# The joining of a DMA-turned SwiGLU tile, moved nine weight units on and tied behind a split in ScalarE's order

## The chip, the cores and the metric

The kernel runs on one core of a Trainium2 chip. The metric is the device time of one execution in microseconds (us). A core has five engines, each with its own queue of instructions that runs in the order in which it was built: TensorE (PE, the matmuls), VectorE (DVE), ScalarE (ACT), GpSimd (POOL) and SyncE (SP, which here only issues DMAs). ScalarE and GpSimd issue DMAs too. An instruction that has to wait on its engine holds up all that stand behind it there.

## The reference

Two decoder layers on a sequence of 256 tokens with a width of 2048. Each layer is a mixer (sparse attention and latent attention side by side, one output projection), a layer norm, a SwiGLU and a second layer norm:

```python
def _swiglu(x, w_gate, w_up, w_down):
    h = jax.nn.silu(jnp.einsum('bsd,df->bsf', x, w_gate)) * jnp.einsum('bsd,df->bsf', x, w_up)
    return jnp.einsum('bsf,fd->bsd', h, w_down)

def reference(x, positions, w_in, ...):
    for i in range(DEPTH):
        mix = _hybrid_mixer(x, positions, w_in[i], ...)
        x = _layer_norm(ALPHA * x + mix, ln1_g[i], ln1_b[i])
        ffn = _swiglu(x, w_gate[i], w_up[i], w_down[i])
        x = _layer_norm(ALPHA * x + ffn, ln2_g[i], ln2_b[i])
    return x
```

All is float32. The hidden width is 5632. The change touches only how the hidden tile of the SwiGLU gets from the gate/up products to the down products.

## The kernel before

**Weight units.** Every matmul takes its operands in two parts, a high part `wh` (rounded to the matmul's format by ScalarE, line 428) and a low part `wl` (what is left, by VectorE, line 429). A weight unit is a tile of 128x1024 (512 KB): two slices of 128 rows with 512 columns each. It is loaded into `raw` by SP, split by `split`, and multiplied: `wh` by the high part of the other operand, `wl` by the high part, `wh` by the low part. `raw` has ten buffers in the SwiGLU, `wh` and `wl` have seven each (`UNITS` 5 and `MORE` 2), so a split waits for the buffer that was used seven units back.

**The SwiGLU.** The 5632 hidden columns are taken in 11 blocks of 512. For a block, `gate_up` makes the gate and up products of 256 tokens by quads of units: a quad stands for a 2x2 group of blocks and is done either plainly or by seven products in place of eight (Winograd's form of Strassen's scheme), for which three units are sums that VectorE or an accumulating DMA makes (lines 1145 to 1159). In some quads the sums are read ready-made from a scratch in HBM. A quad is seven products of six matmuls (`p1 p2 p3 p6 p7 p4 p5`), a block four quads. With the last quad, ScalarE copies product p1 out of its bank into tile `e` (line 1136), and VectorE combines the seven products into `g` and `e` (line 1127). Then `hidden` or `hidden_by_dma` makes silu(gate) times up (lines 1021 to 1026) and the transposed hidden tile `hT` in two parts.

**Turning the tile.** Blocks 0, 2, 4, 6 and 8 of each layer are turned by DMA (`hidden_by_dma`), ten in all. Since the DMA transpose takes elements of two bytes, ScalarE first parts the words into half words (line 1050, into `e`), two DMA transposes are issued on ScalarE's queue (line 1055, from `e` into `g` or `silu`), ScalarE joins the half words again (line 1060, two instructions, into `e`), and a split makes `hT`. Tiles `e` and `silu` (the tag of `g` too) have one buffer each. The other blocks are turned by TensorE (`transpose4`).

**Down.** Ahead of the gate/up of block fc from 2 on, `down_half` multiplies two earlier blocks by half of the columns of `w_down`: eight units, 12 matmuls each. Its sums lie in banks 0 to 3, and ScalarE copies them out with `d` (line 1210), two behind the sixth unit and two behind the eighth. The gate/up products use banks 0 to 3 too: p1 bank 0, p5 bank 1, p6 bank 2, p7 bank 3. So the first product of a block waits until the second pair of `d` has been read out.

**The order.** `tick()` is called once per unit or so, and tasks such as `hidden_by_dma` are generators that are advanced by it: `yield n` means that the next piece is written down n ticks later. The text's order is not the engines' order: a scheduler that models times takes, on each engine, what it holds to be ready, by priority. In the order that it makes, the join of line 1060 stood one or two instructions behind the transposes, whatever was yielded in the text.

Of the kernel before, what the change touches and what calls it, by code (L numbers as in the profile page):

```python
# [28 lines left out]
AF = mybir.ActivationFunctionType  # L29
# [34 lines left out]
BYK = 3  # L64
SOON = 200
FIRSTD = 2
LAND = 7
T2, T2MORE = 4, 6
ALLFROM, SETSFROM, EARLY = 3, 4, 0

# [16 lines left out]
def hybrid_trunk(ctx: ExitStack, tc: tile.TileContext, x, xt_in, pos, w_in, g_cq, g_ckv, w_uq,  # L87
                 w_ukv, w_o, ln1_g, ln1_b, ln1_T, w_gu, w_down, ln2_g, ln2_b, ln2_T, out):
    nc = tc.nc
# [7 lines left out]
    def nm(s):  # L97
        uid[0] += 1
        return f"{s}{uid[0]}"
# [55 lines left out]
    def f(ap):  # L155
        return ap.bitcast(F32)
# [15 lines left out]
    def load_xT(u):  # L172

        if u == 3:
            load_pos()
        elif u == 5:
            gbTs.extend(load_gbT(v[0], True) for v in (ln1_T, ln2_T))
        elif u == 7:
            not_until_now(pos_f)
        s = t2([P, NT, KU, P], "xs")  # L180
        nc.sync.dma_start(s, xt_in[u])
        for t in range(NT):
            split(*x_parts(xT[t], KU * u, KU), s[:, t])
# [45 lines left out]
    def rope_tables():  # L229
# [10 lines left out]
        magic = 1.5 * 2.0 ** 23  # L240
        two_pi = 2.0 * math.pi
        parts, rest = [], two_pi
        for bits in (8, 8, 8):
            e = math.floor(math.log2(rest)) + 1 - bits
# [82 lines left out]
    def some(key, have, more):  # L327

        if phase["name"] == "more":
            phase[key] = phase.get(key, 0) + 1  # L330
            if phase[key] * more % (have + more) < more:
                return phase["pool"], more
        return sb, have
# [18 lines left out]
    latest = {}  # L352
# [7 lines left out]
    def parts(raw, n, own=None, pieces=1):  # L360

        if own is not None:
            wh, wl = own[:, 0], own[:, 1]
        else:
            pool, bufs = some("n", UNITS, MORE)
            wh = pool.tile([P, KU * C], F32R, name=nm("wh"), tag="wh", bufs=bufs)
            wl = pool.tile([P, KU * C], F32R, name=nm("wl"), tag="wl", bufs=bufs)
        latest["wh"] = wh
        for i in range(pieces):
            sl = slice(i * n // pieces, (i + 1) * n // pieces)  # L370
            split(wh[:, sl], wl[:, sl], raw[:, sl])
        return wh[:, :n].rearrange("p (k c) -> p k c", k=KU), wl[:, :n].rearrange("p (k c) -> p k c", k=KU)

    def load_unit(src, n, pieces=1):

        return parts(load_raw(src, n), n, None, pieces)
# [48 lines left out]
            nc.tensor.transpose(psum[:, i * P:(i + 1) * P], s, ident)  # L425

    def split(hi, lo, src):
        nc.scalar.activation(hi, src, AF.Copy)  # L428
        nc.vector.tensor_tensor(lo, src, f(hi), op=ALU.subtract)  # L429

    def xlhs(xT):
        return lambda t, k: tuple(m[:, 0, :] for m in x_parts(xT[t], k, 1))
# [130 lines left out]
    def attend(logits_of, scale, bias, v_of, oh, ol, h0, wait=3):  # L563


        lgs = []
        lp = att()
        logits_of(h0, [[lp[:, j, 0:P], lp[:, j, P:3 * P]] for j in range(2)])
        for t in range(NT):
            n = P * (t + 1)  # L570
            lg = t2([P, 2, n], "lg")
            nc.vector.scalar_tensor_tensor(lg, lp[:, :, t * P:t * P + n], scale,
                                           bias[t].unsqueeze(1).to_broadcast([P, 2, n]), op0=ALU.mult, op1=ALU.add)
            for j in range(2):
                softmax_head(lg[:, j, :], t, n)
            lgs.append(lg)
        yield wait
        prs = []
        for j in range(2):
            tp = trp()  # L580
            transpose4([lgs[0][:, j, :], lgs[1][:, j, 0:P], lgs[1][:, j, P:]], tp)
            pr = t2([P, 3 * P], "pr")
            nc.scalar.activation(pr, tp[:, :3 * P], AF.Copy)
            prs.append(pr)
        yield 1
        op = trp()
        for j, pr in enumerate(prs):
            v0, v1 = v_of(h0 + j)
            ov = op[:, j * S:(j + 1) * S]
            mm(ov, v0, pr[:, 0:S], start=True, stop=False)  # L590
            mm(ov[:, P:], v1, pr[:, S:], start=False, stop=True)
        split(oh.rearrange("p j t -> p (j t)"), ol.rearrange("p j t -> p (j t)"), op)


    def layer(l, xT, norms, last):
# [327 lines left out]
        for c in range(D // C):  # L923
            o = proj([(w_o[l, c, k // KU], range(k, k + KU)) for k in first], olhs, C)
            for t in range(NT):
                sl = xt[t][:, c * C:(c + 1) * C]
# [7 lines left out]
        def last_pass(unit, ks, lhs, then, by, halve=False):  # L934


            us = []
            two = many([P, 2, 2, KU * C])
            for c in range(D // C):
                own = two[:, c] if c < 2 else t8([P, 2, KU * C], F32R, "own")  # L940
                us.append([load_unit(unit(c, ks[0]), KU * C), parts(load_raw(unit(c, ks[1]), KU * C), KU * C, own)])
            for t in range(NT):
                for c in range(D // C):
                    n = C // 2 if halve and t and c == D // C - 1 else C
                    for v in range(0, C, n):
                        o = acc()[:, :n]
                        for i, k0 in enumerate(ks):
                            wh, wl = (w[:, :, v:v + n] for w in us[c][i])
                            for j in range(KU):
                                h, lo = lhs(t, k0 + j)  # L950
                                mm(o, h, wh[:, j, :], start=i == 0 and j == 0, stop=False)
                                mm(o, h, wl[:, j, :], start=False, stop=False)
                                mm(o, lo, wh[:, j, :], start=False, stop=i == len(ks) - 1 and j == KU - 1)
                            tick()
                        sl = xt[t][:, c * C + v:c * C + v + n]
                        with tc.high_priority(offset=SOON):
                            nc.vector.scalar_tensor_tensor(sl, o, by, sl, op0=ALU.mult, op1=ALU.add)
                then(t)
# [54 lines left out]
        def own_words(name):  # L1013

            return phase["pool"].tile([P, NT, C], F32, name=nm(name), tag=name, bufs=1)

        def times_silu(gs, us):

            s = own_words("silu") if isinstance(gs, list) else gs
            for t in range(NT):  # L1020
                nc.scalar.activation(s[:, t, :], gs[t] if isinstance(gs, list) else gs[:, t, :], AF.Silu)
            if isinstance(us, list):
                for t in range(NT):
                    nc.vector.tensor_tensor(s[:, t, :], s[:, t, :], us[t], op=ALU.mult)
            else:
                nc.vector.tensor_tensor(s, s, us, op=ALU.mult)
            return s
# [11 lines left out]
        def words(v):  # L1039

            return v.rearrange("p t c -> p (t c)")

        def hidden_by_dma(gs, us, hT):


            s = times_silu(gs, us)
            e = own_words("e") if isinstance(us, list) else us
            yield 1
            for t in range(NT):
                nc.scalar.activation(e[:, t, :].bitcast(U16).rearrange("p (h c) -> p h c", h=2),  # L1050
                                     s[:, t, :].bitcast(U16).rearrange("p (c h) -> p h c", h=2), AF.Copy)
                yield 1
            turned = words(s).bitcast(U16).rearrange("p (k t) -> p k t", t=S)
            for t in range(NT):
                nc.scalar.dma_start_transpose(turned[:, :, t * P:(t + 1) * P], e[:, t, :].bitcast(U16))
                yield 1
            yield LAND
            whole = words(e).bitcast(U16).rearrange("p (w h) -> p h w", h=2)
            for h in range(2):
                nc.scalar.activation(whole[:, h, :], turned[:, 4 * h:4 * h + 4, :].rearrange("p k t -> p (k t)"), AF.Copy)  # L1060
                yield 1
            split(hT[:, 0], hT[:, 1], words(e).rearrange("p (k t) -> p k t", t=S))

# [169 lines left out]
        def spawn_hidden(fc, g, u):  # L1233
            hT = t8([P, 2, 4, S], F32R, "hT")
            held.append((fc, hT, spawn(hidden_by_dma(g, u, hT) if by_dma(fc) else
                                       hidden(g, u, hT, 3, 2 if fc + 1 < FIRSTD else 4))))
# [103 lines left out]
```

## Time and profile before

| what | us |
|---|---|
| median of 3 runs | 2234.0 (2231.7 to 2241.35) |
| the profiled execution | 2222.58 |
| its span, first to last instruction | 2220.8 |
| TensorE busy in it | 2135.7 |
| VectorE busy | 1862.9 |
| ScalarE busy | 1351.8 |
| mean granted TensorE clock | 0.984 |

Waits are listed as "who waited <- what released it: us in total, times, longest". In a timeline a row is start, duration, engine, line, operation, out <- in; behind it in brackets the idle time of the engine just ahead and what ended it. ACTq is a DMA issue on ScalarE's queue, PEld a weight load of TensorE. In a window row the columns are the stretch, its length, then for PE, PEld, DVE, ACT and POOL the busy time and number of instructions, the granted TensorE clock, the DMA engines' busy share and GB/s.

### The profile page before, as it was taken

How to read it: one execution, taken by the hardware profiler on the slowest of the kernel's cores; microseconds unless marked ns; L12 is line 12 of the kernel's file. 1: busy time of each engine (PE TensorE's matmuls, PEld its weight loads, DVE VectorE, ACT ScalarE, POOL GpSimd, SP SyncE). 2: the span in 40 equal slices, each digit the busy share in tenths (PEclk: the TensorE clock that was granted, in tenths of full speed). 3: DMA queues.
4: the chain of work that ended last, by engine and by line, in shares of the span. 5: the costliest groups of instructions: out<-in, count | busy, mean ns of one | idle time of the engine just before them, and what ended most of it. 6: DMA issues, size and time to landing. Idle time of an engine off the chain costs nothing.

```text
span 2220.8 us, 28336 instructions
## 1 busy us (share of the span) xinstructions
PE 2135.7 (96%) x9862; PEld 1766.8 (80%) x9862; DVE 1862.9 (84%) x2349; ACT 1351.8 (61%) x1732; POOL 334.5 (15%) x527
## 2 busy tenths in 40 slices
PE   9999999999998989989999999999999989899898
PEld 7888888878786868878888888888778868688686
DVE  7697767899897979989867967679989979799897
ACT  6555545666775656666655554466666756566763
POOL 1223220110111100110013122101111111110111
PEclk9999999999999999999999999999999999999999
DMA  8688787689889888988667887867889998989894
GB/s 306 217 294 285 278 309 264 180 240 272 242 278 222 276 235 282 289 240 248 208 180 259 293 302 270 313 213 221 241 245 277 285 217 264 231 278 277 240 308 127
DMA packets 183888, 566.59 MB, mean 255 GB/s; under 512 B 39377, under 2 KB 39681, under 8 KB 183105
## 3 DMA queue, kind: packets, MB, share of 16 engines
q1 hardware_dynamic: 110736, 398.38, 51.2%
q0 software_dynamic: 51600, 160.77, 28.4%
q10 hardware_dynamic: 21408, 5.64, 2.7%
q8 instruction: 77, 1.26, 0.2%
q14 instruction: 67, 0.54, 0.1%
HBM read 506.51 MB, written 31.46 MB: 242 GB/s over the span
## 4 chain that ended last, share of the span: by engine, by line
PE 74%; DVE 9%; DMA 7%; ACT 5%; issue 5%; ACTq 0%; POOL 0%; SPq 0%; DVEq 0%; POOLq 0%
PE acc L392 8%; PE acc L393 8%; PE acc L394 8%; PE gu_p L1085 5%; PE gu_p L1087 5%; PE gu_p L1088 5%; PE acc L1203 4%; PE acc L1204 4%; DMA g<-e 4%; PE acc L1202 4%; DVE wl L429 4%; PE gu_c L1085 3%; PE gu_c L1087 3%; PE gu_c L1088 3%; ACT wh L428 2%
## 5 line engine op out<-in xcount | busy, mean ns | idle before, releaser
L429 DVE TENSOR_TENSOR wl<-raw,wh 128x1024 fp32r<-128x1024 f32 (+2 forms) x925 | 1091.5, 1213 | 269.6 <-ACT wh L428 267.3
L428 ACT ACTIVATE wh<-raw 128x1024 fp32r<-128x1024 f32 (+2 forms) x925 | 948.4, 1050 | 575.3 <-PE acc L394 145.5
L392 PE MATMUL acc<-wh,xhl 128*128 128x512 f32 (+1 forms) x756 | 297.8, 395 | 0.0
L394 PE MATMUL acc<-wh,xhl 128*128 128x512 f32 (+1 forms) x756 | 292.4, 387 | 0.0
L393 PE MATMUL acc<-wl,xhl 128*128 128x512 f32 (+1 forms) x756 | 291.9, 386 | 0.0
L1203 PE MATMUL acc<-wl,hT 128*128 128x512 f32 x640 | 249.7, 390 | 1.1 <-DVE wl L429 1.1
L1202 PE MATMUL acc<-wh,hT 128*128 128x512 f32 x640 | 249.5, 391 | 0.5 <-ACT wh L428 0.5
L1204 PE MATMUL acc<-wh,hT 128*128 128x512 f32 x640 | 249.4, 390 | 0.0
L392 PEld LDWEIGHTS acc<-wh,xhl 128*128 128x128 f32 x756 | 142.1, 188 | 29.9 <-issue 3.3
L394 PEld LDWEIGHTS acc<-wh,xhl 128*128 128x128 f32 x756 | 142.0, 188 | 27.3
L393 PEld LDWEIGHTS acc<-wl,xhl 128*128 128x128 f32 x756 | 142.2, 188 | 26.3 <-DVE wl L429 1.1
L1211 POOL DMA_DIRECT2D x<-d x80 | 68.3, 890 | 486.7 <-ACT d L1210 485.8
L1203 PEld LDWEIGHTS acc<-wl,hT 128*128 128x128 f32 x640 | 120.2, 188 | 26.9 <-DVE wl L429 2.5
L1202 PEld LDWEIGHTS acc<-wh,hT 128*128 128x128 f32 x640 | 120.2, 188 | 25.5 <-ACT wh L428 0.9
L1204 PEld LDWEIGHTS acc<-wh,hT 128*128 128x128 f32 x640 | 120.2, 188 | 24.9
L1087 PE MATMUL gu_c<-wl,xhl 128*128 128x512 f32 x336 | 133.9, 398 | 0.9 <-DVE wl L429 0.8
L1085 PE MATMUL gu_c<-wh,xhl 128*128 128x512 f32 x336 | 134.0, 399 | 0.0
L1088 PE MATMUL gu_c<-wh,xhl 128*128 128x512 f32 x336 | 132.7, 395 | 0.0
L1085 PE MATMUL gu_p<-wh,xhl 128*128 128x512 f32 x152 | 63.7, 419 | 64.6 <-ACT d L1210 64.6
L1087 PE MATMUL gu_p<-wl,many 128*128 128x512 f32 x240 | 94.1, 392 | 2.9 <-DVE wl L429 2.8
L1085 PE MATMUL gu_p<-wh,many 128*128 128x512 f32 x240 | 93.8, 391 | 0.2
L1088 PE MATMUL gu_p<-wh,many 128*128 128x512 f32 x240 | 93.5, 390 | 0.0
(311 smaller groups left out, 3871.7 us busy)
## 6 DMA issues: line engine op xcount, KB each, us to landing
raw<-in_w_gate_dram SPq DMA_DIRECT2D x176, 512.0 KB, 5.6
raw<-in_w_down_dram SPq DMA_DIRECT2D x176, 512.0 KB, 7.4
raw<-in_w_in_dram SPq DMA_DIRECT2D x144, 512.0 KB, 5.5
sum<-in_w_up_dram POOLq DMA_DIRECT2D x124, 512.0 KB, 7.2
raw<-in_w_up_dram SPq DMA_DIRECT2D x100, 512.0 KB, 5.9
raw<-in_w_o_dram SPq DMA_DIRECT2D x64, 512.0 KB, 6.1
q<-q POOLq DMA_DIRECT2D x56, 512.0 KB, 4.6
raw<-q SPq DMA_DIRECT2D x56, 512.0 KB, 6.6
```

The source lines that it names most:

```text
L392: mm(o[t][:, :n], h, a, start=first, stop=False)
L393: mm(o[t][:, :n], h, b, start=False, stop=False)
L394: mm(o[t][:, :n], l, a, start=False, stop=final)
L428: nc.scalar.activation(hi, src, AF.Copy)
L429: nc.vector.tensor_tensor(lo, src, f(hi), op=ALU.subtract)
L1085: mm(o[name], h, a, start=name not in begun, stop=False)
L1087: mm(o[name], h, b, start=False, stop=False)
L1088: mm(o[name], l, a, start=False, stop=end)
L1202: mm(o[c][t], h, wh[:, j, :], start=begin, stop=False)
L1203: mm(o[c][t], h, wl[:, j, :], start=False, stop=False)
L1204: mm(o[c][t], lo, wh[:, j, :], start=False, stop=end)
L1211: nc.gpsimd.dma_start(xt[t][:, c * C:(c + 1) * C], d, accum_op=ALU.add)
```

## The change

`split` returns its ScalarE instruction, `parts` keeps the one of the newest weight unit, and each of the two joins gets an order edge on ScalarE that puts it behind that instruction. The edge sets the order on the engine and adds no semaphore. The wait that is yielded between the transposes and the join grows from 7 ticks to 9.

```diff
-LAND = 7
+LAND = 9
@@ parts
         for i in range(pieces):
             sl = slice(i * n // pieces, (i + 1) * n // pieces)
-            split(wh[:, sl], wl[:, sl], raw[:, sl])
+            latest["high"] = split(wh[:, sl], wl[:, sl], raw[:, sl])
@@
     def split(hi, lo, src):
-        nc.scalar.activation(hi, src, AF.Copy)
+        high = nc.scalar.activation(hi, src, AF.Copy)
         nc.vector.tensor_tensor(lo, src, f(hi), op=ALU.subtract)
+        return high.ins
@@ hidden_by_dma
             yield LAND
             whole = words(e).bitcast(U16).rearrange("p (w h) -> p h w", h=2)
             for h in range(2):
-                nc.scalar.activation(whole[:, h, :], turned[:, 4 * h:4 * h + 4, :].rearrange("p k t -> p (k t)"), AF.Copy)
+                with tc.issue_after(latest["high"]):
+                    nc.scalar.activation(whole[:, h, :], turned[:, 4 * h:4 * h + 4, :].rearrange("p k t -> p (k t)"), AF.Copy)
                 yield 1
```

In the changed kernel lines behind the edits are two higher: the join is L1062, the copies `d` L1212, the copy of p1 L1138, the transposes L1056, the parting L1051.

ScalarE, layer 0, where the tile of block 6 is turned (`e_7148`, `g_7149`) while the down step ahead of block 7 runs (`d` from `acc_7234` on) and its gate/up begins (`wh_7407` is the first product's unit). Before:

```order
L1055 DMA_TRANSPOSE g_7149<-e_7148 128x8x128 x2
L428 ACTIVATE wh_7429<-raw_7405 128x1024
L1060 ACTIVATE e_7148<-g_7149 128x1024 x2
L428 ACTIVATE wh_7441<-raw_7401 128x1024
L1210 ACTIVATE d_7350<-acc_7234 128x512
L428 ACTIVATE hT_7230<-e_7148 128x1024
L1210 ACTIVATE d_7353<-acc_7235 128x512
L428 ACTIVATE wh_7453<-sum_7398 128x1024
L428 ACTIVATE wh_7465<-raw_7403 128x1024
L1210 ACTIVATE d_7392<-acc_7274 128x512
L1210 ACTIVATE d_7395<-acc_7275 128x512
```

And now, from the second pair of `d` on (the two transposes stand above it, with four splits and the first pair of `d` between):

```order
L1212 ACTIVATE d_7392<-acc_7274 128x512
L1212 ACTIVATE d_7395<-acc_7275 128x512
L428 ACTIVATE wh_7476<-raw_7405 128x1024
L428 ACTIVATE wh_7496<-raw_7490 128x1024
L428 ACTIVATE wh_7506<-raw_7492 128x1024
L428 ACTIVATE wh_7516<-raw_7494 128x1024
L428 ACTIVATE wh_7527<-raw_7490 128x1024
L1062 ACTIVATE e_7148<-g_7149 128x1024
L428 ACTIVATE wh_7539<-sum_7487 128x1024
L428 ACTIVATE wh_7550<-raw_7492 128x1024
L1062 ACTIVATE e_7148<-g_7149 128x1024
```

The two joins stood ahead of the four copies `d`; now they stand in the second quad of block 7, behind the unit of its fourth product and behind that of its sixth, and the high part of `hT` three rows after the second. The seven other places where blocks 2 to 8 are turned look alike, in both layers.

ScalarE, layer 0, where the tile of block 0 is turned (`e_4254`, `silu_4249`), at the end of block 1's gate/up and the start of the first down step (`wh_4617`, `wh_4635`, `wh_4655` and `wh_4687` are its units). Before, the two joins and the high part of `hT` stood right behind the transposes, near the start of that gate/up, and at its end stood:

```order
L428 ACTIVATE wh_4562<-sum_4503 128x1024
L428 ACTIVATE wh_4548<-raw_4506 128x1024
L1136 ACTIVATE e_4512<-gu_p_4347 128x512
L428 ACTIVATE wh_4617<-raw_4615 128x1024
L428 ACTIVATE wh_4574<-raw_4508 128x1024
L1021 ACTIVATE g_4513<-g_4513 128x512
```

Now:

```order
L428 ACTIVATE wh_4546<-raw_4505 128x1024
L1062 ACTIVATE e_4254<-silu_4249 128x1024
L428 ACTIVATE wh_4617<-raw_4615 128x1024
L428 ACTIVATE wh_4571<-raw_4507 128x1024
L1062 ACTIVATE e_4254<-silu_4249 128x1024
L428 ACTIVATE wh_4584<-raw_4509 128x1024
L428 ACTIVATE hT_4248<-e_4254 128x1024
L428 ACTIVATE wh_4635<-raw_4633 128x1024
L428 ACTIVATE wh_4655<-raw_4653 128x1024
L428 ACTIVATE wh_4687<-raw_4685 128x1024
L1138 ACTIVATE e_4511<-gu_p_4347 128x512
```

The copy of p1 into the next tile `e` (L1136 before, L1138 now), which needs the one buffer that the join writes, now stands behind the joins, the high part of `hT` and six splits that it stood ahead of. On TensorE the first down step begins with other sums (bank 0's ahead of bank 2's), and 47 of the 48 matmuls on its first four units stand ahead of the transposes of block 1's tile, where 37 did. Layer 1 looks alike.

## The prediction

> **What bounds the kernel now.** I read the page first. TensorE is busy for nearly the whole span, and no other engine is as full:
>
> ```profile
> span 2220.8 us, 28336 instructions
> PE 2135.7 (96%) x9862; PEld 1766.8 (80%) x9862; DVE 1862.9 (84%) x2349; ACT 1351.8 (61%) x1732; POOL 334.5 (15%) x527
> PE acc L392 8%; PE acc L393 8%; PE acc L394 8%; PE gu_p L1085 5%; PE gu_p L1087 5%; PE gu_p L1088 5%; PE acc L1203 4%; PE acc L1204 4%; DMA g<-e 4%; PE acc L1202 4%; DVE wl L429 4%; PE gu_c L1085 3%; PE gu_c L1087 3%; PE gu_c L1088 3%; ACT wh L428 2%
> ```
>
> The third line is the chain that ended last, by line. One entry in it is no computing: the DMA transposes that turn the SwiGLU tile. The list of waits says who stood still for them (columns: who waited, on what, us in total, times, longest):
>
> ```profile
> PEld gu_p L1085 <- ACT d L1210: 67.9, 8, 11.1
> PE gu_p L1085 <- ACT d L1210: 64.6, 8, 10.6
> ACT e L1060 <- DMA g<-e: 54.5, 8, 9.7
> ACT e L1060 <- DMA silu<-e: 2.0, 2, 1.3
> PE gu_p L1087 <- DVE wl L429: 3.8, 5, 1.1
> ```
>
> TensorE waits 8 times for ScalarE's copy out of a down bank, and ScalarE waits 8 times for a transpose to land before the join; beyond these 64.6 us TensorE's next largest wait in the list is 3.8 us. The timelines of one of the 8 places (start, us, engine; down step of blocks 4 and 5, then gate/up of block 7) show that the two are one event:
>
> ```profile
> 806.01 5.41 ACTq L1055 DMA_TRANSPOSE g<-e  x2
> 811.47 1.06 ACT L428 ACTIVATE wh<-raw 128x1024 fp32r<-128x1024 f32 x1 [4.54 <-PE acc L1204]
> 821.67 2.53 ACT L1060 ACTIVATE e<-g 128x1024 uint16<-128x1024 uint16 x2 [9.14 <-DMA g<-e]
> 825.00 0.57 ACT L1210 ACTIVATE d<-acc 128x512 f32<-128x512 f32 x1
> 828.80 1.06 ACT L1210 ACTIVATE d<-acc 128x512 f32<-128x512 f32 x2
> ...
> 799.83 0.39 PE L1204 MATMUL acc<-wh,hT 128*128 128x512 f32 x1
> 818.87 0.39 PE L1204 MATMUL acc<-wh,hT 128*128 128x512 f32 x1
> 829.42 0.79 PE L1085 MATMUL gu_p<-wh,xhl 128*128 128x512 f32 x1 [10.17 <-ACT d L1210]
> 830.02 0.63 PE L1087 MATMUL gu_p<-wl,xhl 128*128 128x512 f32 x1
> 833.83 0.40 PE L1087 MATMUL gu_c<-wl,xhl 128*128 128x512 f32 x1
> 834.30 0.39 PE L1085 MATMUL att<-wh,few 128*128 128x512 f32 x1
> ```
>
> The join stands in ScalarE's queue ahead of the four copies out of the down banks. It waits for the turned tile until 821.67, 15.7 us after the first issue. The second pair of copies, whose bank 0 the next product needs, comes at 828.80. TensorE ended its down products at 819.26 and stands for 10.17 us. The step of the blocks between, with no join ahead, is the control: the first product follows with no wait.
>
> ```profile
> 758.09 0.60 ACT L1210 ACTIVATE d<-acc 128x512 f32<-128x512 f32 x1 [0.25 <-PE acc L1204]
> 759.25 0.39 PE L1085 MATMUL gu_p<-wh,xhl 128*128 128x512 f32 x1
> ```
>
> **The eight waits.** The change puts the join behind the split of the newest weight unit, nine units on. The order shows it 14 rows behind the transposes instead of two, and behind all four copies. So what the copies waited for is gone: 64.6 us of TensorE idle. With it goes a slow restart. Products start 0.227 us apart ahead of it (84 starts from 799.83 to 818.87), but after the stall 0.43 apart. From 829.42 to 834.30 twelve start intervals take 4.88 us where 12 x 0.227 = 2.72 would do: 2.16 us lost. The first and the last of the eight:
>
> ```profile
> 563.31 0.50 PE L1085 MATMUL gu_p<-wh,xhl 128*128 128x512 f32 x1 [4.34 <-ACT d L1210]
> 567.76 0.40 PE L1085 MATMUL att<-wh,few 128*128 128x512 f32 x1
> ...
> 2064.42 0.79 PE L1085 MATMUL gu_p<-wh,xhl 128*128 128x512 f32 x1 [9.24 <-ACT d L1210]
> 2069.58 0.40 PE L1085 MATMUL att<-wh,few 128*128 128x512 f32 x1
> ```
>
> That is 4.45 and 5.16 us for the same twelve, a loss of 1.7 and 2.4; at 2.0 each, 16 us for eight. [...]
>
> Gross gain: 64.6 + 16 = 80.6 us.
>
> **Does the join find its data at its new place?** It stands behind the eleventh gate/up product's split. A weight buffer comes free seven units back, so this split waits for the fourth product to end: 819.26 + 4 x 6 x 0.227 = 824.7, plus the split's 1.0, so 825.7. The data landed by 821.67, 4 us earlier. Behind the join TensorE then holds up to seven products, 7 x 1.36 = 9.5 us of work. The landing is no steady number:
>
> ```profile
> g<-e ACTq DMA_TRANSPOSE x16, 13.2
> silu<-e ACTq DMA_TRANSPOSE x4, 4.9
> raw<-in_w_gate_dram SPq DMA_DIRECT2D x176, 512.0 KB, 5.6
> raw<-in_w_down_dram SPq DMA_DIRECT2D x176, 512.0 KB, 7.4
> DMA to landing us min/median/max: 4.7/11.8/15.2
> ```
>
> These are us from issue to landing, medians by kind, and for the transposes the range. From the first issue at 806.01 the join has 19.7 us before it waits at all, and some 29 before TensorE starves. I cost the wait at nothing; its cover is this margin. If the landing slid by ten, ScalarE would idle some 6 us here, inside the 9.5.
>
> **What is queued behind the join now.** Splits of the second and third quad, and through them VectorE. The join itself is no new work (two of 1.34 us, a high part of 1.04, a low part of 1.22 on VectorE), only later:
>
> ```profile
> L1060 ACT ACTIVATE e<-g x16: 1313/1340/1376, 555.5 to 2057.9; 128x1024 uint16<-128x1024 uint16 x16
> L428 ACT ACTIVATE hT<-e x10: 1040/1044/1057, 446.2 to 2060.5; 128x1024 fp32r<-128x1024 f32 x10
> L429 DVE TENSOR_TENSOR hT<-e,hT x10: 1217/1220/1226, 447.5 to 2062.4; 128x1024 fp32r<-128x1024 f32 x10
> ```
>
> The high part now stands behind the splits of 15 of the 28 gate/up products, and the turned tile is needed only in the down step behind the last: 13 x 1.36 = 18 us later at least. SP issues no transpose; the transposes stay where they were on ScalarE's own queue.
>
> **VectorE and the DMA without the stall.** A pair of blocks, one window with a stall and one without:
>
> ```profile
> 690.00:757.00 67.00, 60.58 (x263) 50.10 (x264) 62.56 (x58) 46.24 (x52) 9.34 (x12) 0.92 0.84 256
> 757.00:822.00 65.00, 62.26 (x275) 51.26 (x273) 53.59 (x50) 38.81 (x42) 5.88 (x8) 1.00 0.97 262
> 740.00:750.00 10.00, 10.00 (x50) 8.37 (x49) 10.00 (x10) 4.74 (x6) 0.00 (x0) 1.00 0.99 373
> ```
>
> Third busy column: VectorE, 62.56 + 53.59 = 116.2 of 132 us. The pair loses about 8.8 + 2.1 = 10.9, so 121.1 is left and VectorE is at 96%. It must idle some of the rest, because it can run only seven units ahead. Bytes: (67 x 256 + 65 x 262)/121.1 = 282 GB/s, where a window of 10 us reached 373. So the DMA has room and VectorE has hardly any. Bounds: nothing lost, or half of the gain given back in the last quad, where VectorE also combines the products. In the control it keeps up, so I take near the low end: 0.6 us in each of eight, 5 us.
>
> **The first block of each layer.** Here the join had nearly no wait (2.0 us in two), and moving it costs. Tiles e and silu have one buffer each, and the next block's combination is written into them; its copy out of p1 must follow the late join. Before:
>
> ```profile
> 446.32 1.23 DVE L429 TENSOR_TENSOR wl<-raw,wh 128x1024 fp32r<-128x1024 f32 x1 [2.13 <-ACT wh L428]
> 466.90 0.58 ACT L1136 ACTIVATE e<-gu_p 128x512 f32<-128x512 f32 x1
> 481.76 1.21 DVE L1026 TENSOR_TENSOR g<-g,e 128x1024 f32<-128x1024 f32 x1
> 483.35 1.03 PE L425 MATMUL tr<-ident,g 128*128 128x128 f32 x8
> ```
>
> In the changed order two joins, the high part and six splits (2.7 + 1.0 + 6 x 0.97) stand ahead of that copy that stood behind it: it moves 9.5 us, and the chain to 481.76 with it, to about 491.3; the tile is done at 492.5. TensorE's order puts 47 of the step's first 48 down products ahead of the transposes, where it had 37: 10 more, 2.3 us, so it would be there at 485.6. So 6.9 us are open, less what VectorE gains earlier, 2.13 idle behind the join and 1.22 of the low part: 3.5 to 6.9 per layer, plus up to 2 for a slow restart. Below that, a gain of up to 3 is excluded by nothing if the chain is covered. I take 4.5 twice: 9 us.
>
> **Sum.** 80.6 - 5 - 9 = 67 us. The profiled execution took 2222.58 us (2220.8 and 1.8 around it) and would take 2156. The runs' median, 2234.0, lies 11 us higher; the same 67 us off it gives **2167 us**.
>
> **Rivals.**
> A, the stall turns into VectorE's: with it at 96% TensorE waits in the last quads and half comes back. For it: 116.2 of 121.1. Against: the control passes at 1.00 clock with no such wait. 2234 - 40 + 9 = 2203.
> B, no change: the idle has another owner. The waits name DMA, and the copies follow the join within 4 us, which speaks against; it would leave 2234 - 0 + 9 = 2243 or, with the joins' places as before, 2234. [...]
> C, slower: without the stall the weight loads press on, the transposes starve beside them and land so late that the tied join holds the splits. It costs more than before when a landing passes 29 + 12 = 41 us, at all eight places; at 45 us it is 16 x 8 + 16 = 144 in place of 81: 2234 + 63 + 9 = 2306. Against: the longest landing is 15.2.
>
> **Chances.** Forecast 0.74 (own range 2150 to 2190), A 0.18, B 0.05, C 0.03. This kernel tells about 0.5% (11 us) from no change. Faster: the forecast and A, 0.92; same 0.05; slower 0.03. The range runs from 2148 (80.6 plus the small gain of the first blocks) to 2203, A's time.
>
> **What will show it.** ScalarE's wait at the join for g<-e near zero, and TensorE's wait for d, 64.6 us, gone, with no product 0.43 us apart there; the DMA gone from the chain. Two TensorE waits of 2 to 6 us near the first block's down step, for e or the low part of its weights. VectorE's idle time down by some 60 us. If TensorE's waits for wl grow past 20 us, A is right; if the join still waits, the margin of 4 us was wrong.

## The result

The changed kernel takes 2151.03 us (median of four runs, 2150.27 to 2151.9), the kernel before 2232.85 in the runs beside it (four, 2226.02 to 2241.35). The ratio is 0.9632 with a 95% interval of 0.9598 to 0.9666: 81.8 us off. The profiled execution of the changed kernel took 2151.9 us, that of the kernel before 2222.58, so that the two traces lie 70.7 us apart, and not 81.8. The forecast was 2167 (2148 to 2203): the direction and the mechanism hold, and 16 us more came off.

From the page of the changed kernel: span, busy times, and the chain that ended last by engine.

```profile
span 2150.1 us, 28337 instructions
PE 2122.9 (99%) x9862; PEld 1758.4 (82%) x9862; DVE 1861.8 (87%) x2349; ACT 1350.9 (63%) x1732; POOL 334.4 (16%) x527
PE 76%; DVE 12%; issue 5%; ACT 4%; ACTq 1%; DMA 1%; POOL 0%; DVEq 0%; SPq 0%; POOLq 0%
```

The transposes have left the chain: DMA is 1% of it, where `g<-e` alone was 4%. TensorE is busy 99% of the span where it was 96%. Its own busy time fell by 12.8 us with the same 9862 matmuls, and the mean granted clock rose from 0.984 to 0.997. That is a net figure: the slow restarts behind the eight waits are gone, and two new ones have come at the first blocks (both are sized further down). All of TensorE's waits above 1 us in sum, but for one of 1.6 us near the start that the kernel before has too:

```profile
PE gu_p L1087 <- ACT d L1212: 4.7, 6, 1.2
PE acc L1204 <- DVE e L1129: 2.9, 2, 1.8
PE gu_p L1089 <- DVE wl L429: 1.7, 3, 0.9
PE acc L1204 <- ACT wh L428: 1.6, 1, 1.6
PE gu_p L1087 <- ACT wh L428: 1.3, 2, 0.8
PE acc L1204 <- ACT e L1138: 1.3, 1, 1.3
```

The first line is what is left of the 64.6 us in eight waits: 4.7 in six. Over all of the list TensorE's idle time before an instruction went from 74.0 to 16.7 us, 57.3 less; with the 12.8 us of busy time this is 70.1 of the 70.7. ScalarE's list has no wait for `g<-e` left. The same place that the prediction walked through (down step of blocks 4 and 5, then block 7), on ScalarE and with TensorE's first product of block 7 and its eighteenth:

```profile
791.37 6.01 ACTq L1056 DMA_TRANSPOSE g<-e  x2
797.43 1.06 ACT L428 ACTIVATE wh<-raw 128x1024 fp32r<-128x1024 f32 x1 [5.14 <-PE acc L1206]
800.98 1.06 ACT L428 ACTIVATE wh<-raw 128x1024 fp32r<-128x1024 f32 x1 [2.49 <-DVE raw L1147]
801.95 1.06 ACT L1212 ACTIVATE d<-acc 128x512 f32<-128x512 f32 x2
804.80 1.08 ACT L1212 ACTIVATE d<-acc 128x512 f32<-128x512 f32 x2
813.11 1.37 ACT L1062 ACTIVATE e<-g 128x1024 uint16<-128x1024 uint16 x1
...
805.44 0.50 PE L1087 MATMUL gu_p<-wh,xhl 128*128 128x512 f32 x1 [0.83 <-ACT d L1212]
809.45 0.39 PE L1090 MATMUL att<-wh,few 128*128 128x512 f32 x1
```

The copies `d` follow the splits, the first join comes 21.7 us behind the first issue and waits for nothing, and TensorE stands 0.83 us instead of 10.17. From the product at 805.44 to the one at 809.45 seventeen starts take 4.01 us, 0.236 each: no slow restart. What still makes `d` late stands in the first three rows. The issue of the two transposes holds ScalarE's queue for 6.01 us, and the split behind it starts when the issue ends, at 797.43. VectorE makes that unit's low part at 798.52 and only then, at 799.66, the sum (L1147) that the next split waits for; the first pair of copies follows that split at 801.95. That the issue is the cause is tested below, with the transposes on another queue.

### The profile page after: what moved, and what is told of

Its sections match the earlier page's. It is cut to its first block, busy times and chain, and to the rows that moved or that the text cites. A ratio compares the mean times of both kernels' runs of the same rounds, so it can differ in the third digit from the quotient of the medians.

```text
span 2150.1 us, 28337 instructions
## 1 busy us (share of the span) xinstructions
PE 2122.9 (99%) x9862; PEld 1758.4 (82%) x9862; DVE 1861.8 (87%) x2349; ACT 1350.9 (63%) x1732; POOL 334.4 (16%) x527
## 4 chain that ended last, share of the span: by engine, by line
PE 76%; DVE 12%; issue 5%; ACT 4%; ACTq 1%; DMA 1%; POOL 0%; DVEq 0%; SPq 0%; POOLq 0%
PE acc L392 8%; PE acc L393 8%; PE acc L394 8%; DVE wl L429 6%; PE acc L1204 5%; PE acc L1205 5%; PE acc L1206 5%; PE gu_p L1087 5%; PE gu_p L1089 5%; PE gu_p L1090 5%; PE gu_c L1090 3%; PE gu_c L1089 3%; PE gu_c L1087 3%; ACT wh L428 2%; PE tr L425 2%
## 5 line engine op out<-in xcount | busy, mean ns | idle before, releaser
L1087 PE MATMUL gu_c<-wh,xhl 128*128 128x512 f32 x336 | 130.8, 389 | 0.0
L1090 PE MATMUL gu_c<-wh,xhl 128*128 128x512 f32 x336 | 130.7, 389 | 0.0
L349 POOL DMA_DIRECT2D sum<-in_w_up_dram x62 | 52.6, 849 | 297.5 <-DMA sum<-in_w_up_dram 297.4
```

Of the source, the lines that this page charges most:

```text
L1087: mm(o[name], h, a, start=name not in begun, stop=False)
L1090: mm(o[name], l, a, start=False, stop=end)
```

## The experiments

Two questions: is it the place of the joins that counts, and what is left between the changed kernel and one without the turning?

### The wait of nine units alone

```diff
-LAND = 7
+LAND = 9
```

The kernel before with this line alone, without the tie.

> The yielded wait of 9 alone, without the tie: the scheduler's order puts the joins as in the kernel before, two instructions behind the transposes. Theory P: as before, ratio to before 0.995 to 1.005, eight TensorE waits for d of 60 to 85 us in all. Rival W (the longer yielded wait does it): 2145 to 2160.

Measured: 2230.78 us (ten runs, 2221.77 to 2236.35) against 2230.59 (13 runs) of the kernel before, ratio 1.0005 (0.9987 to 1.0023). TensorE's wait for `d` in it:

```profile
PE gu_p L1085 <- ACT d L1210: 71.3, 8, 13.0
```

The number in the text does nothing while the scheduler may place the join as it likes; the stall is all there. The gain is the tie's.

### The tie with shorter waits

The changed kernel with `LAND` at 7 and at 5.

> The tie alone, with the yielded wait left at 7. Theory P (place): what matters is that the joins stand behind all four copies out of the down banks. Here they still do (first join right behind the seventh gate/up unit, two units earlier than with 9), so TensorE's eight waits stay gone and the time stays within 8 us of the changed kernel, 2143 to 2155. ScalarE reaches the join at about the time of the last down product plus 1.3 us, some 14 us after the first issue, so it may wait 0 to 3 us each time for a landing of 13 to 17 us, at most 20 us in all, with seven products behind it as cover. In the first block the copy of p1 stands four instructions earlier, so 1 to 4 us may be gained there. Rival L (landing): nine units are needed, the join holds the splits and a third of the stalls returns, 2170 or more.

> The tie with a yielded wait of 5: the joins land between the copies out of the down banks, the first ahead of the second copy of the first pair, the second ahead of both copies of the second pair. Theory P (place): the stall is back, since the second pair stands behind a join that waits until the landing: 5 to 8 us in each of eight places, 2190 to 2225. Rival T (the tie itself, any place a few units on): as the changed kernel, 2145 to 2160.

Measured: 2157.86 us with 7 (2153.76 to 2165.25; ratio 0.9693, 0.9658 to 0.9727) and 2202.18 with 5 (2197.75 to 2212.97; ratio 0.9887, 0.9851 to 0.9924). With 5 the tie puts the joins in among the copies `d`, here the first join behind the first copy; one of the places, and TensorE's wait for `d` in that kernel:

```profile
680.39 0.58 ACT L1212 ACTIVATE d<-acc 128x512 f32<-128x512 f32 x1
684.21 1.34 ACT L1062 ACTIVATE e<-g 128x1024 uint16<-128x1024 uint16 x1 [3.24 <-DMA g<-e]
685.42 0.56 ACT L1212 ACTIVATE d<-acc 128x512 f32<-128x512 f32 x1
...
PE gu_p L1087 <- ACT d L1212: 48.7, 8, 10.1
```

The same transposes, the same tie, and 48.7 us of the stall stand again when three of the four copies are queued behind a join. So it is the order of join and copies that decides, as the expectation had it. With 7, where the joins still stand behind all four copies, TensorE waits 4.8 us for `d` and four joins wait 2.7 us in all for their tile. The time lies 3 us above the theory's range and 12 below the rival's. Whether the two units less cost anything isn't shown: the changed kernel's 2151.03 was measured at another time, and the intervals of the two ratios overlap.

### No transposes

```diff
-                nc.scalar.dma_start_transpose(turned[:, :, t * P:(t + 1) * P], e[:, t, :].bitcast(U16))
...
-    nc.scalar.activation(whole[:, h, :], turned[...], AF.Copy)
+    nc.scalar.activation(whole[:, h, :], ident..., AF.Copy)
```

The kernel before without its twenty transposes, and then the changed kernel likewise; the joins read a constant tile. Both leave out the turned data of ten SwiGLU tiles.

> The kernel before without the ten pairs of DMA transposes, the joins at their old place reading a constant tile instead (so the SwiGLU's result is left out and the join waits for no DMA). Theory P: the wait for the landing is the whole cost of the old place: the eight stalls vanish and the first blocks keep their early join, 2140 to 2152, at or a little below the changed kernel. Rival Q (the joins' own 2.7 us ahead of the copies cost too): some 2 to 3 us stay at each of eight places, 2165 to 2180.

> The changed kernel without the twenty DMA transposes; the joins, at their new places, read a constant tile. It leaves out the turned data of ten SwiGLU tiles, nothing else. The kernel before without its transposes took 2133.2. Theory (the 18 us that the changed kernel stays above that are mostly the transposes themselves: their issue holds ScalarE's queue for some 5 us ten times, which makes the copies d about 1 us late, and they take room from the weight loads; the later place of the joins adds the 2 to 4 us of the first blocks): 2134 to 2141. Rival (the late joins and their splits cost the 18 us, through VectorE): 2145 to 2152.

Measured: 2133.24 us (2132.58 to 2133.9) with the joins at the old place, 2141.84 (2140.3 to 2142.85) at the new one. In neither is there a wait for `d`. The first is 7 us faster than its theory had it, and the rival, by which the joins' own work ahead of the copies costs 2 to 3 us at each of eight places, fell. The late joins seem to cost 8.6 us by the medians, 7.7 by the two spans. But the two were measured at different times, and their ratios to the kernel before (0.9571, 0.9546 to 0.9596, against 0.9589, 0.9569 to 0.961) overlap, so that the difference rests on where the traces show it. Most of it lies at the first blocks. These are the fourth copies of the first down step of layer 0, of the last one of layer 0 and of the first of layer 1, with the old place and then, in the second fence, with the new:

```profile
493.97 0.60 ACT L1210 ACTIVATE d<-acc 128x512 f32<-128x512 f32 x1 [0.76 <-PE acc L1204]
...
1040.25 0.60 ACT L1210 ACTIVATE d<-acc 128x512 f32<-128x512 f32 x1 [0.76 <-PE acc L1204]
...
1553.80 0.60 ACT L1210 ACTIVATE d<-acc 128x512 f32<-128x512 f32 x1 [0.76 <-PE acc L1204]
```

```profile
497.06 0.60 ACT L1212 ACTIVATE d<-acc 128x512 f32<-128x512 f32 x1 [0.76 <-PE acc L1206]
...
1043.07 0.60 ACT L1212 ACTIVATE d<-acc 128x512 f32<-128x512 f32 x1 [0.76 <-PE acc L1206]
...
1560.00 0.60 ACT L1212 ACTIVATE d<-acc 128x512 f32<-128x512 f32 x1 [0.76 <-PE acc L1206]
```

Up to the first down step the new place loses 3.1 us, and between the last down step of layer 0 and the first of layer 1 another 3.4 (516.9 against 513.55; 1.7 of it is a slow restart of TensorE at 1535.3); the four other tiles of layer 0 lose nothing (546.01 against 546.28 us between the first two of these copies). The changed kernel lies 10 us above its own version without transposes (2151.75, measured together with it). That is what the transposes still cost behind the hidden landing: more than the 4.7 us of waits for `d`. So of the 18 us that the expectation speaks of the medians give about half to the transposes and half to the late joins; the time is 0.8 us above the range of the theory, which had given the late joins 2 to 4.

### The first block's joins left where they were

```diff
-            yield LAND
+            first = isinstance(us, list)
+            yield 7 if first else LAND
...
+                    if not first:
+                        tied.enter_context(tc.issue_after(latest["high"]))
```

> The changed kernel, but the tile of block 0 of each layer (the two places with hardly any wait before) is joined as it was before the change: no tie, seven units. Theory (the late join of the first block is what makes the two TensorE waits of 1.6 to 1.8 us at the first down step, and moves its fourth copy 1.9 us later in each layer): 2 to 6 us below the changed kernel of the same call, 2145 to 2149, and the waits for e and wh at the first down steps (1.28, 1.82, 1.58, 1.10) gone. Rival (those waits are paid by another one in the same place, so the first block was free): within 1.5 us of the changed kernel, 2149.5 to 2152.5.

> The changed kernel itself, as the baseline of this call and for its spread: 2151 us, 2149.5 to 2153. Its runs should lie within 3 us of each other, where those of the kernel before lie 10 to 20 apart, if the spread of the kernel before comes from the landing that its copies waited for.

Measured: 2156.52 us (2153.05 to 2159.4; ratio 0.9653, 0.9633 to 0.9673) against 2151.75 (2148.17 to 2156.91; 0.9634, 0.961 to 0.9658) of the changed kernel, measured together with it. The theory of 2 to 6 us of gain fell. The intervals overlap, so that it isn't shown to be slower either. TensorE at the first block, untied and then, in the second fence, in the first profile of the changed kernel (the last row is for a later section):

```profile
456.12 0.50 PE L1092 MATMUL gu_p<-wl,many 128*128 128x512 f32 x1 [0.66 <-DVE wl L429]
459.52 0.50 PE L1092 MATMUL gu_c<-wl,xhl 128*128 128x512 f32 x1 [0.35 <-DVE wl L429]
461.79 0.50 PE L1092 MATMUL gu_p<-wl,many 128*128 128x512 f32 x1 [0.61 <-DVE wl L429]
468.61 0.50 PE L1092 MATMUL gu_p<-wl,few 128*128 128x512 f32 x1 [1.09 <-DVE wl L429]
```

```profile
464.68 0.50 PE L1089 MATMUL gu_p<-wl,few 128*128 128x512 f32 x1 [0.91 <-DVE wl L429]
469.22 0.50 PE L1089 MATMUL gu_p<-wl,few 128*128 128x512 f32 x1 [0.17 <-DVE wl L429]
471.92 0.50 PE L1204 MATMUL acc<-wh,hT 128*128 128x512 f32 x1 [1.28 <-ACT e L1138]
472.63 0.50 PE L1205 MATMUL acc<-wl,hT 128*128 128x512 f32 x1 [0.20 <-DVE wl L429]
483.05 0.53 PE L1204 MATMUL acc<-wh,hT 128*128 128x512 f32 x1 [1.82 <-DVE e L1129]
486.77 0.39 PE L1204 MATMUL acc<-wh,hT 128*128 128x512 f32 x1
```

At its early place the join waits 1.6 us in the two layers for its tile, and TensorE waits 2.71 us for low parts in layer 0; at its late place it waits 4.38. The kernel before has the early waits too, 2.90 us. Both places pay, at other lines. The fourth copy `d` of the first down step says the same: it starts at 497.14 us untied and at 497.71 in the changed kernel measured together with it, and from the last down step of layer 0 to that copy in layer 1 it is 518.37 against 517.96 us. So the first blocks cost much the same at either place. The 5 us by which the untied profile is longer lie between those copies, in the other tiles of layer 0 (561.02 against 554.01): ScalarE waits 7.7 us there for one sum of weight units that landed late, and one issue of two transposes holds it for 9.5 us, with a wait of 4.3 us for `d` behind it.

The changed kernel's runs lie within 1.6 us in the first four and within 8.7 in these, where the seven of the kernel before lie within 8.3 (13.1 and 16.8 at two other times). So the expectation of 3 us did not hold, and the change has not made the time steady; with the transposes on SP's queue, below, the runs lie within 1.9 and 2.2. In this second profile of the changed kernel TensorE waits at other places too, and ScalarE once 5.0 us for such a sum, which the first profile doesn't have; what makes that sum late in some executions wasn't tried.

### The transposes on SP's queue

```diff
-                nc.scalar.dma_start_transpose(turned[:, :, t * P:(t + 1) * P], e[:, t, :].bitcast(U16))
+                nc.sync.dma_start_transpose(turned[:, :, t * P:(t + 1) * P], e[:, t, :].bitcast(U16))
```

The changed kernel with this line, measured twice.

> The changed kernel with the two DMA transposes of each tile issued on SP's queue, amid the weight loads, in place of ScalarE's. Theory (their issue on ScalarE's queue is what makes the copies d late): TensorE's waits for d fall from 4.7 us to under 1 and the time to 2140 to 2149. Rival (SP stands at the transposes until their tile is parted, and the weight loads behind them come late, or the loads beside them are what costs): TensorE's waits for wh and wl grow by 5 us or more and the time is 2152 to 2175.

> The changed kernel with the transposes on SP's queue once more, as the baseline for the two others of this call: 2138 to 2141.5.

Measured: 2139.7 us (four runs, 2138.91 to 2140.82; ratio 0.9579, 0.9561 to 0.9596), and 2141.84 (2139.91 to 2142.08; 0.9595, 0.9581 to 0.9608) the second time; each lies 0.3 us outside its expected range. This beats both kernels: 12 us under the changed one measured together with the first, with intervals that don't overlap, and not above the changed kernel without transposes (2141.84, measured together with the first too). Its ScalarE at the place of above, and its issues and landings (out <- in, queue, count, KB, median us to landing):

```profile
785.65 1.99 ACT L1051 ACTIVATE e<-g 128x1024 uint16<-128x1024 uint16 x2
790.07 1.07 ACT L428 ACTIVATE wh<-raw 128x1024 fp32r<-128x1024 f32 x1 [1.48 <-PE acc L1206]
794.87 1.25 ACT L1212 ACTIVATE d<-acc 128x512 f32<-128x512 f32 x2
799.59 0.60 ACT L1212 ACTIVATE d<-acc 128x512 f32<-128x512 f32 x1 [0.30 <-PE acc L1206]
...
raw<-in_w_down_dram SPq DMA_DIRECT2D x176, 512.0 KB, 7.7
g<-e SPq DMA_TRANSPOSE x16, 5.6
silu<-e SPq DMA_TRANSPOSE x4, 4.2
```

The changed kernel's own transposes, on ScalarE's queue:

```profile
g<-e ACTq DMA_TRANSPOSE x16, 13.9
silu<-e ACTq DMA_TRANSPOSE x4, 4.5
```

Nothing holds ScalarE between the parting and the splits, the second pair of copies waits for TensorE and not the other way round, and TensorE's list has no wait for `d` any more. The rival fell: TensorE's waits for `wh` and `wl` are 3.1 us where they were 5.6, and the loads on SP's queue land about as fast as before, those of `w_gate` in 5.6 us and those of `w_down` in 7.7 (5.6 and 7.4 in the kernel before). And the transposes themselves land in 5.6 us instead of 13.9.

### The transposes on SP's queue, the joins at the old place

The same line in the kernel before, and in the version whose first blocks are untied.

> The kernel before, its joins ahead of the copies d and untied, with the twenty DMA transposes issued on SP's queue in place of ScalarE's. In the changed kernel that edit cut the landing of the transposes from 13.2 us (median) to 5.5. Theory (the stall was the late landing and nothing else; the place of the join matters only as long as the tile is late): ScalarE's wait at the join and TensorE's wait for d both fall under 10 us in sum, and the time to 2131 to 2145, the 2133 of the kernel before without transposes being the floor. Rival (a join in ahead of the copies holds them however soon the tile lands, since the first of two transposes has to wait for the parting and lands 4 us on): 30 us or more of waits for d stay, 2165 to 2200.

> The kernel with the transposes on SP's queue, and the tile of block 0 of each layer joined as before the change (no tie, seven units), the other four tiles of a layer tied. Theory (the late joins cost 3.1 and 2.4 us at the two first blocks, as the fourth copies d of the first down steps stand in the runs with SP's transposes and with none): 4 to 6 us below the kernel with all ten tied and SP's transposes, 2133 to 2136. Rival (the first block's joins cost as much where they stood, as with the transposes on ScalarE's queue): within 2 us of it, 2138 to 2142.

Measured: 2165.03 us (2161.17 to 2167.49; ratio 0.9701, 0.9685 to 0.9718) for the first, which lies between theory and rival, at the rival's edge. Its waits, and two of its eight places:

```profile
PE gu_p L1085 <- ACT d L1210: 22.2, 8, 7.5
ACT e L1060 <- DMA g<-e: 37.9, 8, 9.5
...
556.28 2.53 ACT L1060 ACTIVATE e<-g 128x1024 uint16<-128x1024 uint16 x2 [9.50 <-DMA g<-e]
564.05 0.79 PE L1085 MATMUL gu_p<-wh,xhl 128*128 128x512 f32 x1 [7.49 <-ACT d L1210]
...
682.55 2.59 ACT L1060 ACTIVATE e<-g 128x1024 uint16<-128x1024 uint16 x2 [3.14 <-DMA g<-e]
690.39 0.50 PE L1085 MATMUL gu_p<-wh,xhl 128*128 128x512 f32 x1 [1.20 <-ACT d L1210]
```

Six of the eight waits shrink to 0.7 to 2.8 us, as a landing in about 5 us would have it (5.3 in the median of the twenty). At the first place of each layer the transposes land late all the same (11.6 us is the longest) and 7.5 and 6.5 us remain. The other queue alone, its landing and its issue together, gives 65 us of the gain, the tie another 23 to 25 beside it: tied behind the copies, the joins of blocks 2 to 8 wait for nothing and hold nothing up.

The second is 2139.78 us (2139.11 to 2140.7; ratio 0.959, 0.9577 to 0.9603) against 2141.84 with all ten tied: within 2 us, as the rival had it. Its two first joins wait 7.6 us for `silu<-e`. The fourth copy `d` of the first down step starts at 497.2, against 497.1 and 498.5 in the two profiles with all ten tied and 494.0 in the kernel before without transposes. Once more both places of the first join pay.

### A second profile of the kernel before

> The kernel before once more, for a second profile of it. Theory (its executions spread because the landing of its transposes does, and the profile that the prediction was made from was a mild one): an execution near 2233 has 70 to 78 us of waits for d, one near 2222 has 62 to 68. Rival (the spread is elsewhere): 62 to 68 us whatever the time.

Measured: 2235.64 us, and

```profile
PE gu_p L1085 <- ACT d L1210: 76.9, 8, 13.0
```

The theory holds: 12.3 us more of waits for `d` than in the prediction's profile, in an execution that took 13.1 us longer. The version with `LAND` at 9 and no tie fits between: 71.3 us of waits in an execution of 2228.22. These are three executions, one profile each.

## Why the prediction came out as it did

**What bounds the kernel.** Right. The join ahead of the copies is the cause: undone in part (`LAND` at 5) the waits return, and without transposes they are gone with the joins at either place.

**The eight waits.** The step was right and its size was read from a mild execution. The prediction took 64.6 us from a profile of 2222.58 and subtracted it from a median of 2234.0. An execution at that median has about 76 us of it, an estimate between the two profiles with 71.3 and 76.9 us on either side. The sum should have stayed on its own execution: 2222.58 - 67 = 2156 was given in the prediction, and 2151.9 was measured, 4 us off. The other 11.4 us of the error are the step from 2156 to 2167. Of the 64.6 us the change took 59.9; the 4.7 left come with the issue of the transposes on ScalarE's queue (on SP's they are gone), which the prediction saw in the row at 806.01 and only counted as time on the way to the landing.

**The slow restarts.** Right. Measured as the prediction did it, twelve start intervals against 12 x 0.227, all eight restarts of that execution lost 16.2 us, and the six short waits that are left lose 0.8: 15.4 us gone, where 16 were put down. The busy time fell by less, 12.8 us, because two slow restarts have come at the first blocks. Behind the wait of 1.82 at 483.05 nine start intervals, up to the row at 486.77, take 3.72 us where 2.04 would do: 1.7 lost, and as much in layer 1 behind two waits of 1.58 and 1.10. So the waits of 0.4 to 1.2 us at the eight places cost next to nothing (0.236 us a start behind the one of 0.83), while a longer one can cost a slow restart. In the second profile a wait of 1.81 at 585.28 loses 1.7 again, while 1.79 at 482.62 and 1.92 at 1754.88 lose next to nothing. What decides between them isn't known.

**The join at its new place.** Right: 21.7 us behind the issue against the 19.7 that were worked out. No join waits in the first profile. In the second, where the longest landing was 21.0 us, one waits 1.2: the margin is real and not large.

**VectorE.** The 5 us weren't paid: TensorE's waits for `wl` in the gate/up products fell from 4.6 us (3.8 and 0.8) to 1.7. VectorE's wait for the high parts shrank instead, in the kernel before and then in the changed one:

```profile
DVE wl L429 <- ACT wh L428: 268.3, 160, 9.5
...
DVE wl L429 <- ACT wh L428: 193.4, 138, 5.5
```

That is 74.9 us less. All of VectorE's idle time (span less busy time) fell by 69.6, where some 60 were forecast. Rival A would have needed it to be TensorE that waits.

**The first block.** The step that failed most: 9 us were put down. The fourth copy `d` of the first down step starts at 499.71 us where it started at 497.81, and in layer 1 the stretch from the last down step of layer 0 to that copy takes 519.7 us where it took 517.8. That is 1.9 twice, 3.8 in all, and a slow restart of 1.7 is in each. In the second profiles, where the changed kernel has no slow restart at these two places, no shift can be made out (497.71 and 517.96 us against 497.07 and 519.1 in the kernel before). The chain behind tile `e` was found rightly, and TensorE waits for it at 471.92 and 483.05, 1.28 and 1.82 us where two waits of 2 to 6 were forecast. What was mis-sized is how far the chain moves. The prediction put the copy of p1 9.5 us later, from 466.90 to about 476.4, and the last instruction of the chain, the multiplication of silu(gate) by up, from 481.76 to about 491.3. In the changed kernel they start here:

```profile
471.28 0.59 ACT L1138 ACTIVATE e<-gu_p 128x512 f32<-128x512 f32 x1
...
483.94 1.23 DVE L1027 TENSOR_TENSOR g<-g,e 128x1024 f32<-128x1024 f32 x1
```

That is 4.4 and 2.2 us later. In the kernel before ScalarE stood idle shortly ahead of that copy (2.97 us at 465.93, 1.31 at 459.06), which fits that only part of the work put ahead of it delays it. The early place has a price too: with the join there TensorE waits 2.90 us for four low parts in layer 0 of the kernel before, which the prediction had only as time that VectorE gains. Without transposes the move costs 6.5 us, nearer to the 9; with them most of that is paid at the old place too.

**The sum.** In its own execution the terms were 64.6 + 16 - 5 - 9 = 66.6; measured were 59.9 (waits for `d`) + 12.8 (busy time: 15.4 of restarts less 2.6 of slower work elsewhere) - 2.6 (all other waits, 9.4 to 12.0) = 70.1. Of the 14 charged (5 and 9) about 5 was paid; the 9 that weren't outweigh the 4.7 of waits that stayed.

**Rivals.** A and C did not come. B is refuted: 59.9 of the 64.6 us of waits for `d` went when the joins moved behind the copies. Why the landing was slow is a question of its own. On SP's queue a transpose lands in the time of a load, 5.6 us against 5.6 to 7.7, but it moves half the bytes (128x8x128 elements of two bytes, 256 KB, against 512), so that by bytes it isn't as fast; on ScalarE's queue, in this kernel, it takes 13.9 us. The prediction took the landing as given, and more than half of it came with the queue.

## What to carry to other kernels

Where an in-order engine has to wait for a DMA, look at what is queued behind the waiting instruction, and tie it behind the work that others wait for (here TensorE's waits for `d` went from 64.6 us to 4.7); a delay in the text is worth nothing if a scheduler is free to place the instruction (here 2230.78 us against 2230.59). Then ask what the issue of that DMA costs the engine that issues it, and try another queue: here it gave 12 us more. And subtract a stall from the execution in which it was measured, not from a median, when the stall is what makes the executions differ.

## What was not expected of the hardware

The same transposes of the same tile land in 13.9 us (median) from ScalarE's queue and in 5.6 from SP's, in the midst of the same loads. Those of the first block, `silu<-e`, land in 4.5 and 4.2, and on ScalarE's queue those of block 2 in 6.4 to 8.6, where those of blocks 4 to 8 take 12.4 to 17.0; so the queue alone doesn't make them slow. The issue is also shorter on SP's queue. These are the rows of the transposes' line, for the changed kernel and then with SP's queue (duration of an issue in ns: min, median, max):

```profile
L1056 ACTq DMA_TRANSPOSE g<-e x16: 1247/2759/5107, 547.6 to 1983.7; - x16
```

```profile
L1056 SPq DMA_TRANSPOSE g<-e x16: 1237/1616/3577, 545.1 to 1971.6; - x16
```

Why the transposes land sooner from the queue that also carries the loads isn't settled; no run took it apart.
